# Low halves of 24 weight panels by a negation and an accumulating transfer, in place of VectorE's subtraction

## The chip, the cores and the metric

The program runs on one core of a Trainium2 chip. The metric is the device time of one execution, in microseconds (us); the kernel before takes 2033.01 us, the median of three runs (2031.76 to 2034.62).

## What is computed

A two-layer encoder over 512 tokens of width 1024. Layer 0 mixes by attention, layer 1 by a gated delta rule; around each mixer stand two half-step gated feed-forward networks (FFN), with an RMS norm ahead of every part. The change touches the mixer of layer 1 alone, cut here to its core:

```
def odd_mixer(h, w_in, conv_w, a_log, dt_bias, norm_w, w_out):
    # h: (1, 512, 1024); 8 heads of 128
    q, k, v, z, b, a = split(h @ w_in)
    q, k, v = silu(causal_depthwise_conv([q, k, v], conv_w))   # 4 taps
    q, k = l2_normalize(q), l2_normalize(k)
    g, beta = decay(a, a_log, dt_bias), sigmoid(b)
    o = gated_delta_rule_chunked(q, k, v, g, beta)             # scan over chunks
    return (rms_norm(o, norm_w) * silu(z)) @ w_out
```

## The kernel before

Every dense product runs on TensorE (PE) in three passes over numbers split in two: a high half that is the number rounded to the engine's format, and a low half, the rest. xh·wh, xl·wh and xh·wl are summed. Activations are kept split as `xnh` and `xnl`; weights are split on the way. `panel` (L163 to L177) fetches one panel of weights, 128 partitions by 1024 numbers (512 KB), from DRAM into a buffer `raw` by a transfer issued on SyncE (SP), copies it to `wh` on ScalarE (ACT, L174), which rounds, and subtracts on VectorE (DVE, L175): `wl = raw - wh`. There are three buffers each of `raw`, `wh` and `wl`, so the copy of a panel waits until PE has used the panel three before it, and the next load into a `raw` waits for the subtraction that read it.

The input projection of the delta rule goes by four pairs of heads. For each pair and each of the sections k, q and v `gdn_proj` calls `proj_steps`, which takes two panels (upper and lower half of the 1024 rows, called a and b below; k1b is the second panel of k of pair 1) and runs 24 matrix products with each, into two accumulators `mm`. `gdn_conv` (L919 to L937) then scales the result into `cx` on DVE (L926), takes the first tap into `cy` on ACT (L929), three more on DVE (L931), and the activation into `c` on ACT (L934, L937). The freeing of `cx` and `cy` goes in turn through ACT and DVE.

Beside the projections run the steps of the delta rule, of one pair while the next pair's panels are multiplied: `gdn_keys` (sums of squares on L962, scaled keys `kdec` on ACT, L972, products `iu`), and `gdn_base`, which inverts 32-wide triangular blocks on GpSimd (POOL): `iu` goes to DRAM and back as `lb` (issued by ACT, L1025), 31 steps of a product (L1037) and a subtraction (L1040) follow on POOL, and the result `rr` goes out by four transfers `rd<-rr`, issued by ACT (L1043), and back as `r` (L1046). There are four of these, base(0) to base(3), one for each pair; each head is scaled at the end by a factor `rs` (a power, POOL) on ACT (`on`, L1133).

Each engine works through its own list in order, and an instruction that issues a transfer waits at its place in that list, holding up what stands behind it. PE's list is written by hand as interleaved steps; on the other engines a scheduler orders the instructions by its estimate of when they are ready.

Of the kernel before, what the change touches and what calls it, by code (L numbers as in the profile page):

```python
# [10 lines left out]
F32 = mybir.dt.float32  # L11
F32R = mybir.dt.float32r
AF = mybir.ActivationFunctionType
ALU = mybir.AluOpType
# [3 lines left out]
D = 1024  # L18
# [70 lines left out]
class Ordered:  # L89


    def __init__(self, tc):
        self.tc, self.engine = tc, tc.nc.tensor
# [8 lines left out]
class Trunk:  # L102
# [4 lines left out]
    def __init__(self, ctx, tc):  # L107
        self.tc = tc
        self.nc = tc.nc
        self.const = ctx.enter_context(tc.tile_pool(name="const", bufs=1))  # L110
        self.xp = ctx.enter_context(tc.tile_pool(name="xp", bufs=1))
        self.wp = ctx.enter_context(tc.tile_pool(name="wp", bufs=4))
        self.np_ = ctx.enter_context(tc.tile_pool(name="np", bufs=2))
        self.ps = ctx.enter_context(tc.tile_pool(name="ps", bufs=2, space=bass.MemoryType.PSUM))
        self.dram = ctx.enter_context(tc.tile_pool(name="dr", bufs=1, space=bass.MemoryType.DRAM))
        self.ahead, self.pending, self.pin = [], [], None
        self.te = self.nc.tensor
        self.x = [self.xp.tile([P, T], F32, name=f"x{c}") for c in range(KC)]
        self.consts()
# [43 lines left out]
    def panel(self, src, a, b):  # L163

        if self.ahead:
            return self.ahead.pop()
        nc = self.nc
        raw = self.wp.tile([P, 1024], F32, tag="raw", name="raw", bufs=NRAW)
        v = raw[:, :a * b].rearrange("p (a b) -> p a b", b=b)
        nc.sync.dma_start(v, src)  # L170
        h = self.wp.tile([P, 1024], F32R, tag="wh", name="wh", bufs=NSPL)
        l = self.wp.tile([P, 1024], F32R, tag="wl", name="wl", bufs=NSPL)
        n = a * b
        nc.scalar.copy(out=h[:, :n], in_=raw[:, :n])  # L174
        nc.vector.tensor_tensor(l[:, :n], raw[:, :n], h[:, :n].bitcast(F32), op=ALU.subtract)  # L175
        return (h[:, :n].rearrange("p (a b) -> p a b", b=b),
                l[:, :n].rearrange("p (a b) -> p a b", b=b))  # L177

# [132 lines left out]
            pass  # L311
        return ps

    def proj_steps(self, ps, w, col, mk=None, cut=1):

        ps.extend(f() for f in mk or (self.mm_ps, self.mm_ps))
        n = T // cut
        for kh in range(2):
            h, l = self.panel(self.rows_half(w, kh, col), 4, 256)
            for i in range(cut):  # L320
                t = slice(i * n, (i + 1) * n)
                for j in range(2):
                    s = slice(j * P, (j + 1) * P)
                    for k in range(4):
                        kk = kh * 4 + k
                        xh, xl = self.xn[kk]
                        with self.placed():
                            self.mm3(ps[j][:, t], (h[:, k, s], l[:, k, s]), (xh[:, t], xl[:, t]),
                                     kk == 0 and i == 0, kk == KC - 1 and i == cut - 1)
                        yield  # L330
                    if kh + j and i == cut - 1:
                        self.slot()
        self.pin = None
# [427 lines left out]
    def gdn_proj(self, pool, Ks, sec, p, w_in, conv, half):  # L761

        ps = []
        yield from self.proj_steps(ps, w_in, sec * D + p * 256)
        for j, K in enumerate(Ks):
            tanh = (sec, p) in TANH
            K["qkv"[sec]] = self.gdn_conv(pool, ps[j], sec, 2 * p + j, half if tanh else conv, tanh)
# [436 lines left out]
```

## Time and profile before

| | us |
|---|---|
| median of the runs | 2033.01 |
| the profiled execution | 2032.96 |
| its span in the trace | 2031.2 |
| PE busy in the span | 1999.0 (98%) |
| DVE busy | 1084.6 (53%) |
| ACT busy | 748.3 (37%) |
| POOL busy | 130.9 (6%) |
| projections and delta rule of layer 1 | about 1324 to 1660 of the span |

In the trace a matrix product of 512 columns follows the one before it after some 0.23 us where nothing is waited for. In a timeline row stand the start, the length, engine, line, operation, what it writes and reads, and in brackets how long the engine stood idle before it and what ended that. A row "ACTq" is ACT's queue issuing a transfer. PEclk is the clock that TensorE was granted, as a share of full speed.

### The profile page before, as it was taken

The page shows a single profiled execution, that of the slowest core. Times are in us where ns is not written, and L with a number is a line of the kernel's source. Part 1 is how long each engine was busy: PE and PEld are TensorE (multiplying, and loading weights), DVE is VectorE, ACT ScalarE, POOL GpSimd, SP SyncE. Part 2 cuts the span into 40 slices and gives each one's busy share as a digit, 9 for nine tenths or more (in the row PEclk, how much of TensorE's full clock was granted, in tenths as well). Part 3 has the DMA queues.
Part 4 walks back from the last instruction along what each step waited for, and adds up shares of the span by engine and source line. Part 5 has one row for each costly group of instructions (what it writes and reads, how often), then busy time and mean ns, then how long its engine had stood idle before and what let it go on. Part 6 is the DMA issues. An engine that isn't in the chain of part 4 may idle for free.

```text
span 2031.2 us, 24843 instructions
## 1 busy us (share of the span) xinstructions
PE 1999.0 (98%) x9786; PEld 1667.5 (82%) x9786; DVE 1084.6 (53%) x1752; ACT 748.3 (37%) x1359; POOL 130.9 (6%) x298
## 2 busy tenths in 40 slices
PE   8999999999999999999999999998999999999998
PEld 7888888889888888888888888877877788888887
DVE  6452454597675433444544344478577685443543
ACT  5232233355663222233332232355465453322322
POOL 0000000100000000000000000005432400000000
PEclk9999999999999999999999999999999999999999
DMA  4333333222123333333333333234223233223332
GB/s 157 94 99 98 94 99 98 86 84 73 47 90 103 94 104 94 94 103 94 94 95 102 94 95 103 93 111 115 77 80 92 75 100 104 94 90 97 93 101 76
DMA packets 189866, 192.24 MB, mean 95 GB/s; under 512 B 28546, under 2 KB 165044, under 8 KB 189748
## 3 DMA queue, kind: packets, MB, share of 16 engines
q1 hardware_dynamic: 158916, 182.62, 28.7%
q10 hardware_dynamic: 30832, 8.02, 1.7%
q8 instruction: 77, 1.26, 0.3%
q14 instruction: 41, 0.34, 0.1%
HBM read 185.35 MB, written 5.26 MB: 94 GB/s over the span
## 4 chain that ended last, share of the span: by engine, by line
PE 89%; POOL 5%; DMA 2%; DVE 1%; issue 1%; ACT 1%; ACTq 0%; SPq 0%; POOLq 0%
PE mm L181 10%; PE mm L182 10%; PE mm L183 10%; PE pa L181 9%; PE pa L183 8%; PE pa L182 8%; PE pb L181 8%; PE pb L183 8%; PE pb L182 8%; PE mm L96 4%; POOL tmp L1037 2%; POOL rr L1040 2%; PE pb L96 1%; DMA lb<-iud 1%; DMA iud<-iu 1%
## 5 line engine op out<-in xcount | busy, mean ns | idle before, releaser
L175 DVE TENSOR_TENSOR wl<-raw,wh 128x1024 fp32r<-128x1024 f32 (+1 forms) x348 | 413.2, 1187 | 564.1 <-ACT wh L174 563.1
L174 ACT CAST wh<-raw 128x1024 fp32r<-128x1024 f32 (+1 forms) x348 | 355.6, 1022 | 702.0 <-PE pb L182 279.9
L181 PE MATMUL mm<-xnh,wh 128*128 128x512 f32 (+1 forms) x816 | 316.5, 389 | 0.6 <-ACT wh L174 0.6
L183 PE MATMUL mm<-xnh,wl 128*128 128x512 f32 (+1 forms) x816 | 317.1, 389 | 0.0
L182 PE MATMUL mm<-xnl,wh 128*128 128x512 f32 (+1 forms) x816 | 316.7, 388 | 0.0
L181 PEld LDWEIGHTS mm<-xnh,wh 128*128 128x128 f32 x816 | 154.3, 189 | 31.6 <-ACT wh L174 1.0
L183 PEld LDWEIGHTS mm<-xnh,wl 128*128 128x128 f32 x816 | 154.2, 189 | 30.5 <-issue 0.5
L182 PEld LDWEIGHTS mm<-xnl,wh 128*128 128x128 f32 x816 | 154.3, 189 | 30.4 <-issue 0.2
L181 PE MATMUL pa<-xnh,wh 128*128 128x512 f32 x400 | 156.2, 390 | 0.0
L183 PE MATMUL pa<-xnh,wl 128*128 128x512 f32 x400 | 155.8, 389 | 0.0
L183 PE MATMUL pb<-xnh,wl 128*128 128x512 f32 x400 | 155.7, 389 | 0.0
L181 PE MATMUL pb<-xnh,wh 128*128 128x512 f32 x400 | 155.7, 389 | 0.0
L182 PE MATMUL pa<-xnl,wh 128*128 128x512 f32 x400 | 155.7, 389 | 0.0
L182 PE MATMUL pb<-xnl,wh 128*128 128x512 f32 x400 | 155.7, 389 | 0.0
L226 ACT CAST hid<-hd 128x512 fp32r<-128x512 f32 x88 | 54.5, 620 | 209.0 <-DVE hd L398 209.0
L96 PE MATMUL mm<-xnh,wh 128*128 128x512 f32 x256 | 109.2, 426 | 12.0 <-DVE cx L926 12.0
L392 DVE TENSOR_TENSOR gr<-mm,rb 128x512 f32<-128x512 f32 x80 | 55.2, 691 | 94.7 <-PE mm L183 94.6
L183 PE MATMUL pb<-hid,wl 128*128 128x512 f32 x264 | 102.8, 389 | 0.0
L181 PE MATMUL pa<-hid,wh 128*128 128x512 f32 x264 | 102.7, 389 | 0.0
L182 PE MATMUL pa<-hid,wh 128*128 128x512 f32 x264 | 102.7, 389 | 0.0
L183 PE MATMUL pa<-hid,wl 128*128 128x512 f32 x264 | 102.7, 389 | 0.0
L181 PE MATMUL pb<-hid,wh 128*128 128x512 f32 x264 | 102.7, 389 | 0.0
(308 smaller groups left out, 3365.1 us busy)
## 6 DMA issues: line engine op xcount, KB each, us to landing
raw<-in_ffn_w_gate_dram SPq DMA_DIRECT2D x88, 512.0 KB, 3.6
raw<-in_ffn_w_up_dram SPq DMA_DIRECT2D x88, 512.0 KB, 3.6
raw<-in_ffn_w_down_dram SPq DMA_DIRECT2D x88, 512.0 KB, 3.6
raw<-in_gdn_w_in_dram SPq DMA_DIRECT2D x32, 512.0 KB, 3.9
raw<-in_att_w_in_dram SPq DMA_DIRECT2D x24, 512.0 KB, 3.5
raw<-in_gdn_w_out_dram SPq DMA_DIRECT2D x16, 256.0 KB, 2.7
xr<-in_x_dram SPq DMA_DIRECT2D x4, 512.0 KB, 5.6
raw<-in_att_w_out_dram SPq DMA_DIRECT2D x4, 512.0 KB, 3.4
```

The costliest lines, as they stand in the source:

```text
L96: return self.tc.keep_in_program_order(self.engine.matmul(*args, **kw))
L174: nc.scalar.copy(out=h[:, :n], in_=raw[:, :n])
L175: nc.vector.tensor_tensor(l[:, :n], raw[:, :n], h[:, :n].bitcast(F32), op=ALU.subtract)
L181: self.te.matmul(out, lhsT=lh, rhs=rh, start=start, stop=False)
L182: self.te.matmul(out, lhsT=lh, rhs=rl, start=False, stop=False)
L183: self.te.matmul(out, lhsT=ll, rhs=rh, start=False, stop=stop)
L226: nc.scalar.copy(out=h, in_=src)
L392: nc.vector.tensor_tensor(gr, g[j], self.rb, op=ALU.mult)
L1037: nc.gpsimd.tensor_tensor(p, rr[:, :k, j:j + 1].broadcast_to(sh), lb[:, j, j + 1:].rearrange("p (o m) -> p o m", o=1) .broadcast_to(sh), o ...
L1040: nc.gpsimd.tensor_tensor(rr[:, :k, j + 1:], rr[:, :k, j + 1:], p, op=ALU.subtract)
```

## The change

For the sections q, k and v of the input projection (24 panels: 4 pairs, 3 sections, 2 halves) the subtraction on DVE is left out. ACT writes `-wh` into `wl` (a second pass over the panel), and POOL issues a transfer from SBUF to SBUF that adds `raw` to it. The panels of the gate, of the output projection, of attention and of the FFNs keep the subtraction.

```
 def panel(self, src, a, b):
         nc.scalar.copy(out=h[:, :n], in_=raw[:, :n])
-        nc.vector.tensor_tensor(l[:, :n], raw[:, :n], h[:, :n].bitcast(F32), op=ALU.subtract)
+        if self.by_dma:
+            nc.scalar.activation(l[:, :n], h[:, :n].bitcast(F32), AF.Copy, scale=-1.0)
+            nc.gpsimd.dma_start(l[:, :n].bitcast(F32), raw[:, :n], accum_op=ALU.add)
+        else:
+            nc.vector.tensor_tensor(l[:, :n], raw[:, :n], h[:, :n].bitcast(F32), op=ALU.subtract)
...
-    def proj_steps(self, ps, w, col, mk=None, cut=1):
+    def proj_steps(self, ps, w, col, mk=None, cut=1, by_dma=False):
...
+            self.by_dma = by_dma
             h, l = self.panel(self.rows_half(w, kh, col), 4, 256)
+            self.by_dma = False
...
-        yield from self.proj_steps(ps, w_in, sec * D + p * 256)
+        yield from self.proj_steps(ps, w_in, sec * D + p * 256, by_dma=True)
```

In the changed file the lines of the delta rule stand 7 further down (L1037 is L1044); the negation is L177, the transfer L178. PE's list is the same row for row. DVE's has 24 instructions fewer, ACT's and POOL's 24 more each, and the scheduler has put several rows of ACT and DVE elsewhere.

First place: ACT ahead of the first `kdec` (L972, L979). Before:

```order
L904 ACTIVATE egl<-on 128x4 x2
L174 CAST wh<-raw 128x1024
L901 ACTIVATE du_10341<-du_10341 128x512
L962 ACTIVATE gosq,sk<-pa 128x128 x3
L901 ACTIVATE du_10351<-du_10351 128x512
L907 ACTIVATE kdc<-kdc 128x4x2
L904 ACTIVATE egl<-on 128x4
L962 ACTIVATE gosq,sk<-pa 128x128 x4
L934 ACTIVATE c<-cy 128x512
L904 ACTIVATE egl<-on 128x4
L962 ACTIVATE gosq,sk<-pa 128x128
```

The three rows that follow it are `cy` (L929), the cast of a panel and the first `kdec`. Now, up to the first `kdec`:

```order
L911 ACTIVATE egl<-on 128x4
L969 ACTIVATE gosq,sk<-pa 128x128
L936 ACTIVATE cy<-cx,half 128x512
L969 ACTIVATE gosq,sk<-pa 128x128 x3
L175 CAST wh<-raw 128x1024
L969 ACTIVATE gosq,sk<-pa 128x128
L177 ACTIVATE wl<-wh 128x1024
L969 ACTIVATE gosq,sk<-pa 128x128
L936 ACTIVATE cy<-cx,half 128x512
L941 ACTIVATE c<-cy 128x512
L979 ACTIVATE kdec<-pa,kd 128x128 x4
```

A negation, and one `cy` with its `c` that stood behind, come ahead of `kdec`; the sums of squares are spread among them.

Second place: POOL inside base(0), from its 20th step (75 numbers a partition). Before:

```order
L1037 TENSOR_TENSOR tmp<-rr,lb 128x75
L1040 TENSOR_TENSOR rr<-rr,tmp 128x5x15
L1037 TENSOR_TENSOR tmp<-rr,lb 128x70
L1040 TENSOR_TENSOR rr<-rr,tmp 128x5x14
L1037 TENSOR_TENSOR tmp<-rr,lb 128x65
L1040 TENSOR_TENSOR rr<-rr,tmp 128x5x13
```

Now:

```order
L1044 TENSOR_TENSOR tmp<-rr,lb 128x75
L1047 TENSOR_TENSOR rr<-rr,tmp 128x5x15
L178 DMA wl<-raw 128x1024
L1044 TENSOR_TENSOR tmp<-rr,lb 128x70
L1047 TENSOR_TENSOR rr<-rr,tmp 128x5x14
L1044 TENSOR_TENSOR tmp<-rr,lb 128x65
L1047 TENSOR_TENSOR rr<-rr,tmp 128x5x13
L178 DMA wl<-raw 128x1024
```

The transfers of v1a and v1b stand between the steps; that of q1b stands in the same way after the seventh step, those of q2b, v2a and v2b in base(1), those of k3a (after the 24th step, `rr` of 48 numbers) and k3b in base(2), none in base(3).

Third place: ACT at base(1)'s `rd<-rr`. Before:

```order
L929 ACTIVATE cy<-cx,conv 128x512
L1121 COPY on<-pb 128x128
L1125 ACTIVATE gosr,gss<-on 128x128 x2
L937 ACTIVATE c<-cy 128x512
L174 CAST wh<-raw 128x1024
L1121 COPY on<-pb 128x128 x2
L1125 ACTIVATE gosr,gss<-on 128x128 x2
L1043 DMA rd<-rr 32x8x32 x4
L929 ACTIVATE cy<-cx,conv 128x512
```

Now:

```order
L944 ACTIVATE c<-cy 128x512
L175 CAST wh<-raw 128x1024
L177 ACTIVATE wl<-wh 128x1024
L1128 COPY on<-pb 128x128 x2
L1132 ACTIVATE gosr,gss<-on 128x128 x2
L936 ACTIVATE cy<-cx,conv 128x512
L1128 COPY on<-pb 128x128 x2
L1132 ACTIVATE gosr,gss<-on 128x128
L175 CAST wh<-raw 128x1024
L1132 ACTIVATE gosr,gss<-on 128x128
L1050 DMA rd<-rr 32x8x32 x4
L1140 ACTIVATE on<-on,rs 128x128 x4
```

The `cy` that stood behind the four transfers stands ahead of them now; four scalings `on`, a `c` and another `cy` stand between them and `r<-rd`. At base(0)'s `rd<-rr` ten `cy` of the projections stand ahead in both. At base(2)'s, twelve copies `on` (L1121, now L1128) stand ahead in place of ten.

## Rows read from the trace of the kernel before

**Rows 1.** The page: engine busy times; the two groups of the split.
```profile
PE 1999.0 (98%) x9786; PEld 1667.5 (82%) x9786; DVE 1084.6 (53%) x1752; ACT 748.3 (37%) x1359; POOL 130.9 (6%) x298
...
L175 DVE TENSOR_TENSOR wl<-raw,wh 128x1024 fp32r<-128x1024 f32 (+1 forms) x348 | 413.2, 1187 | 564.1 <-ACT wh L174 563.1
L174 ACT CAST wh<-raw 128x1024 fp32r<-128x1024 f32 (+1 forms) x348 | 355.6, 1022 | 702.0 <-PE pb L182 279.9
```

**Rows 2.** Waits of PE, 1280 to 1680: in total, times, longest.
```profile
PE mm L96 <- DVE cx L926: 12.0, 3, 6.5
PE pa L99 <- ACT on L1133: 3.3, 3, 2.5
PE pa L96 <- ACT kdec L972: 2.6, 1, 2.6
```

**Rows 3.** Stretches: length, PE, PEld, DVE, ACT, POOL busy; PEclk, DMA share, GB/s.
```profile
1360.00:1380.00 20.00, 17.44 (x101) 15.11 (x100) 18.34 (x56) 13.36 (x45) 2.01 (x2) 1.00 0.61 160
...
1400.00:1420.00 20.00, 13.51 (x59) 10.84 (x58) 10.83 (x17) 6.99 (x17) 10.97 (x28) 0.88 0.31 86
...
1460.00:1480.00 20.00, 15.18 (x71) 12.41 (x70) 10.40 (x22) 7.30 (x22) 10.91 (x30) 0.83 0.21 57
```

**Rows 4.** Timeline of ACT: the first `kdec`.
```profile
1367.42 1.14 ACT L972 ACTIVATE kdec<-pa,kd 128x128 f32<-128x128 f32 x4
```

**Rows 5.** Timelines of POOL (base(0): step 1, a slow row, step 20) and ACT behind it.
```profile
1381.34 0.24 POOL L1037 TENSOR_TENSOR tmp<-rr,lb 128x31 f32<-128x31 f32 x1 [14.08 <-DMA lb<-iud]
...
1389.19 1.17 POOL L1040 TENSOR_TENSOR rr<-rr,tmp 128x66 f32<-128x66 f32 x1
...
1399.22 0.66 POOL L1040 TENSOR_TENSOR rr<-rr,tmp 128x75 f32<-128x75 f32 x1
...
1413.12 1.82 ACTq L1043 DMA_DIRECT2D rd<-rr  x4
1415.04 0.72 ACT L929 ACTIVATE cy<-cx,conv 128x512 f32<-128x512 f32 x1 [11.99 <-issue]
```

**Rows 6.** Timeline of PE: first product with v1a's `wl`; the long wait.
```profile
1396.47 0.40 PE L96 MATMUL mm<-xnh,wl 128*128 128x512 f32 x1
...
1417.20 0.80 PE L96 MATMUL mm<-xnh,wh 128*128 128x512 f32 x1 [6.49 <-DVE cx L926]
```

**Rows 7.** Timelines of ACT and PE behind base(1), and PE's next scan.
```profile
1472.25 0.72 ACT L929 ACTIVATE cy<-cx,conv 128x512 f32<-128x512 f32 x1 [9.19 <-DMA rd<-rr]
...
1475.59 0.80 PE L96 MATMUL mm<-xnh,wh 128*128 128x512 f32 x1 [4.82 <-DVE cx L926]
1476.18 0.63 PE L96 MATMUL mm<-xnl,wh 128*128 128x512 f32 x1
1476.61 0.63 PE L96 MATMUL mm<-xnh,wl 128*128 128x512 f32 x1
...
1485.92 0.89 PE L96 MATMUL pb<-t,iu 32*32 32x32 f32 x32
```

**Rows 8.** Timelines in base(2): POOL, DVE; PE's first product with k3a's `wl`.
```profile
1521.28 1.17 POOL L1040 TENSOR_TENSOR rr<-rr,tmp 128x65 f32<-128x65 f32 x1
1526.80 0.28 POOL L1040 TENSOR_TENSOR rr<-rr,tmp 128x48 f32<-128x48 f32 x1
...
1520.99 1.28 DVE L175 TENSOR_TENSOR wl<-raw,wh 128x1024 fp32r<-128x1024 f32 x1 [0.16 <-ACT wh L174]
...
1528.63 0.40 PE L96 MATMUL mm<-xnh,wl 128*128 128x512 f32 x1
```

**Rows 9.** Transfers by kind: times, KB each, median us from issue to landing.
```profile
raw<-in_gdn_w_in_dram SPq DMA_DIRECT2D x32, 512.0 KB, 3.9
...
iud<-iu ACTq DMA_DIRECT2D x8, 256.0 KB, 2.4
...
out_dram<-xt SPq DMA_DIRECT2D x4, 512.0 KB, 2.7
```

**Rows 10.** Timeline of POOL: one operation outside the bases.
```profile
1333.01 1.01 POOL L160 TENSOR_TENSOR rt<-ms,halfFalse 128x4 f32<-128x4 f32 x1 [350.45 <-DVE ms L278]
```

More of the change, by code (lines that the diff above doesn't have):

```diff
@@ L318, in proj_steps @@
         for kh in range(2):
+            self.by_dma = by_dma
             h, l = self.panel(self.rows_half(w, kh, col), 4, 256)
+            self.by_dma = False
             for i in range(cut):
```

## The prediction

> **What bounds the kernel now.** I read the page first, then PE's waits in the projection stage of layer 1, then timelines around each wait. PE is busy for 98% of the span; the split of the weights by ACT (1.02 us a panel) and DVE (1.19 us a panel) runs beside it [rows 1]. So taking 24 subtractions from DVE (24 x 1.19 = 28.5 us) and giving 24 negations to ACT (24 x 1.02, by the cast of the same size, = 24.5 us) is worth nothing by itself. What counts is what it does to PE's few waits in the stage: three behind `cx`, 12.0 us together, three behind `on`, 3.3, one behind `kdec`, 2.6 [rows 2]. The two long ones are of one kind. ACT reaches the issue of `rd<-rr` and stands there until POOL has ended a base; a `cy` behind it starts only then, after an idle time of 12.0 us at base(0) and 9.2 at base(1) [rows 5, 7]; DVE's `cx` waits for the buffer and PE for `cx`, 6.49 and 4.82 us [rows 6, 7]. After each, PE runs slower: the products behind the second follow each other by 1476.61 - 1476.18 = 0.43 us [rows 7] where two before the first wait stand closer than their 0.40 us of length [rows 6] (0.23 us is the usual step), and the granted clock of those stretches is 0.88 and 0.83 [rows 3], the lower of the levels 1.2 and 2.4 GHz for part of them. I count 12 and 13 such products: 12 x 0.2 = 2.4 us and, less the last partial one, 2.3.
>
> POOL is idle for nearly all of the span [rows 1], but not here: it takes from 1381.3 to 1413.1 for base(0) [rows 5], and its list is what the new transfers stand in.
>
> **What a low half costs now.** Until now it is ready 1.2 us after the cast. Now: a negation (1.0), POOL's turn, POOL's own time for the transfer, and the landing. No row shows an accumulating transfer or one that POOL issues. POOL's time: the low bound is ACT's issue, 1.82 us for four, 0.46 each [rows 5]; the high one is a slow operation of POOL, 1.17 [rows 5]; I take 1.0, that of its one-off power operation [rows 10]. The landing: the nearest row is a transfer of the same 512 KB out of SBUF, 2.7 us; 256 KB out of SBUF take 2.4. The high bound is a load of 512 KB and such a store one after the other, 3.9 + 2.7 = 6.6 [rows 9]. The accumulation fetches two streams and writes one, so I take 2 x 2.7 = 5.4 us, with 2.4 and 6.6 for the range. From POOL's turn to a finished `wl` that makes 6.4 us.
>
> A panel whose transfer POOL can take at once is then ready 1.0 + 6.4 - 1.2 = 6.2 us later than now. The spare time between the subtraction's end and PE's first use is 1528.63 - 1522.27 = 6.36 us for k3a [rows 8]; v1a has about as much, the other 22 panels more. So a plain delay of all panels is just hidden, with little left. What is not hidden is POOL's place: a transfer in the middle of a base waits for the steps ahead of it.
>
> **Part by part** (shifts against the profiled execution, 2032.96 us, which lies 0.05 under the median; its span is 1.8 shorter).
>
> *kdec.* Ahead of the first `kdec` [rows 4] ACT now has two negations (one of them far up, in the order of the first place) and a `cy` (0.72) with its `c` (0.6) that stood behind: 2 x 1.02 + 1.3 = 3.3 us more. About half a microsecond of idle time in front takes some; I put +2.8 us on PE's wait, making 5.4. ACT is busy for 13.4 of these 20 us [rows 3], so the low bound is nothing, and the high one 3.3. A wait of 5 us brings the slow products that the 4.82 us wait brings; I take 2.0. Together +4.8. The issue of `iud<-iu` moves less, since what was between the two `kdec` has gone ahead: base(0) starts 1.8 us later, at 1383.1.
>
> *base(0).* Now v1a's transfer stands behind step 20. In the trace this step ends at 1399.22 + 0.66, 18.5 us after the start [rows 5]. One transfer (q1b) stands ahead (+1.0). Two slow operations of POOL go: the one of 1.17 us started 0.3 us after a subtraction of DVE did, as in base(2), where 1.17 at 1521.28 follows a subtraction at 1520.99 [rows 5, 8]; without it I put 0.3, so 0.9 less each, 1.8 for two. The transfer's turn is done at 1383.1 + 18.5 + 1.0 - 1.8 = 1400.8 with 1.0 of its own still to come in the 6.4: `wl` at 1407.2 or so. PE wants it at 1396.47 + 4.8 = 1401.3 [rows 6]: a **new wait of 6.0 us**. The base, with three transfers (+3.0), ends at 1413.1 + 1.8 - 1.8 + 3.0 = 1416.1, so the wait behind `cx`, which ended at 1417.20, would end at 1420.2. PE would come there at 1417.20 - 6.49 = 1410.7, plus 10.8, 1421.5: that wait is gone. The slow products go with it and come with the new one. Running sum: 4.8 + 6.0 - 6.5 = **+4.3**.
>
> *base(1).* In the third place `cy` has gone ahead of `rd<-rr`. The 4.82 us and the 2.3 of slow products go: -7.1. The four `on`, `c` and `cy` that now stand ahead of `r<-rd` make `r` late, and PE comes earlier to the scan that reads `t`, made of `r` (1485.92 [rows 7]). With that scan at 1485.9 + 4.3 - 7.1 = 1483.1 and base(1) done at 1470.4 + 4.3, some 10 us for issue, two transfers (1.7 and 2.9 us of landing), the rows between and the turn of `t` leave 1.4 us of a new wait. Sum: 4.3 - 5.7 = **-1.4**.
>
> *base(2).* k3a's transfer stands behind step 24, which ends at 1526.80 + 0.28 [rows 8]; two slow operations less (1.7) make 1525.3, and `wl` is there at 1531.7 against 1528.63: a new wait of 3.1 us, with 1.5 of slow products. The copies that ACT now does ahead of `rd<-rr` bring `rs` and `on` earlier; of the 3.3 us behind `on` [rows 2] I take back 0.8. Sum: -1.4 + 4.6 - 0.8 = **+2.4**.
>
> *The rest.* base(3) has no transfer. The first panels and those behind the bases find POOL free. `raw` is free one landing later than now, and is not reloaded before some 7 us on. PE's list is the same. That gives 2032.96 + 2.4 = 2035.4, say **2035**, no change that can be measured: 0.2%, 4 us, is about what a measurement of this kernel can tell, so "the same" is 2028.9 to 2037.1.
>
> **Rivals.**
>
> *Cheap and covered: faster, 2028.* The landing is that of a plain store, 2.7 us [rows 9], and ACT's extra work falls into its idle third, so `kdec` costs nothing. base(0) ends 1.2 us later (three transfers less two slow operations), and the `cx` wait with it, which swallows v1a's wait; base(1) gives its 5.7; k3a waits for 1525.3 + 3.7 - 1528.63 = 0.4; `on` gives 0.8. Sum: 1.2 - 5.7 + 0.4 - 0.8 = -4.9. For it speaks that the engines move little at base(0) (share 0.31 [rows 3]); against it, that the new order ahead of `kdec` is plain to see.
>
> The Trainium skill, page "DMA: Bandwidth & Descriptors", section "Anatomy of one DMA — SWDGE (gpsimd) path", fits a transfer issued by GpSimd with 2.0 us plus the bytes by 436 thousand per us; for 512 KB that is an estimate of 3.2 us. No row here shows one. With 3.2 in place of 5.4 and `kdec` as in my forecast, the sum would be -2.6, some 2030, between this rival and the forecast.
>
> *Transfers in each other's way: slower, 2047.* The accumulation shares the DMA engines with the loads of `raw` (the share is 0.61 at 1360 to 1380 [rows 3]). If each lands behind one load, 5.4 + 3.9 = 9.3 us [rows 9], v1a and k3a wait 3.9 us longer each, and a low half comes 10.1 us later than now, more than some eight panels have to spare; three buffers let a group of neighbours wait once, so I estimate 4 us for them. Sum: 2.4 + 7.8 + 4 = +14. It decides from a landing of about 6 us on, where k3a's 6.36 us are used up without POOL's part in it. For it: the thin margin. Against: half of these stretches' DMA time is free.
>
> *The accumulation can't keep up: 2080 and more.* PE uses a panel up in 24 products of 0.23 us, 5.4 us, and three buffers allow about three times that from cast to use. With a landing over 12 us every panel waits, some 2 us or more on 24 panels. Only an operation unlike any row would do that.
>
> **How the numbers follow.** Forecast 0.40 (its own range 2030 to 2039: 0.33 the same, 0.07 slower); cheap 0.27 (0.22 faster, 0.05 the same); in each other's way 0.25; can't keep up 0.08. Faster 0.22, same 0.38, slower 0.40. The range goes from 2025 (the cheap case with `kdec` even a little earlier, and base(1) without its new wait) to 2056 (the crowded case with the estimated part doubled and slow products behind it); the last rival and thin ends are left out.
>
> **What would show it.** DVE has 24 rows of L175's kind less, ACT 24 negations of about 1.0 us. PE's wait behind `kdec` near 5 us; a wait of PE behind v1a's transfer in place of the 6.49 us at 1410.7; none behind `cx` at base(1), a short one behind `t` or `r` after it; one of 3 us at k3a. The landing of `wl<-raw` in the table of transfers decides between the cases: under 3.5 us speaks for the cheap one, over 6 for the crowded one. I would be wrong in kind if POOL's own time for a transfer were several microseconds (the bases would end later by three times that, and PE's waits with them), or if the scheduler's moves on ACT and DVE opened a wait in a place that I took as unchanged, the first panels above all.

## The result

The changed kernel takes 2051.23 us (four runs, 2050.76 to 2051.85) beside 2032.54 (four runs) for the kernel before on the same chip: a ratio of 1.0091, with a 95% interval of 1.0079 to 1.0103. It is slower by 18.7 us. The profiled execution took 2051.85 us; its span in the trace is 2050.1, that of the kernel before 2031.2.

The page of the changed kernel: busy times; the split's two groups; the group that waits for transfers; the software queue, and the new kind of transfer.

```profile
PE 2002.1 (98%) x9786; PEld 1669.6 (81%) x9786; DVE 1058.7 (52%) x1728; ACT 770.9 (38%) x1383; POOL 148.2 (7%) x322
...
q0 software_dynamic: 3456, 12.58, 3.3%
...
L180 DVE TENSOR_TENSOR wl<-raw,wh 128x1024 fp32r<-128x1024 f32 (+1 forms) x324 | 384.0, 1185 | 559.2 <-ACT wh L175 558.5
...
L96 PE MATMUL mm<-xnh,wl 128*128 128x512 f32 x256 | 103.0, 402 | 10.3 <-DMA wl<-raw 10.3
...
wl<-raw POOLq DMA_DIRECT2D x24, 512.0 KB, 5.2
```

Beside [rows 1], DVE has 24 subtractions and 25.9 us less, ACT 24 negations and 22.6 us more, POOL 17.3 us more. PE does the same work. The time went into its waits. PE's waits in the stage (compare [rows 2]): in total, times, longest.

```profile
PE mm L96 <- DMA wl<-raw: 10.3, 4, 7.1
PE pa L96 <- DVE iu L989: 7.5, 1, 7.5
PE pa L99 <- ACT vb L1022: 7.3, 1, 7.3
PE mm L96 <- DVE cx L933: 3.8, 2, 3.4
PE pa L99 <- ACT on L1140: 2.5, 1, 2.5
PE pa L99 <- ACT gosq L1008: 1.8, 1, 1.8
PE pb L96 <- DVE t L1086: 1.4, 2, 0.9
```

With two short ones the list adds up to 35.5 us; before it was 19.8, 17.9 of it in [rows 2]. That is 15.7 of the 18.9 us by which the span grew. The remaining 3.2 are slow products behind the waits: PE's busy time grew by 3.1 us with the same instructions. PE's list is the same in both, so one product can be laid beside itself. The rows of before are in [rows 6 to 8]; here are those of after, with the products behind `kdec`, behind `vb` and behind base(2):

```profile
1372.58 1.65 PE L96 MATMUL pa<-c 128*128 128x128 f32 x6 [7.54 <-DVE iu L989]
...
1411.08 0.80 PE L96 MATMUL mm<-xnh,wl 128*128 128x512 f32 x1 [7.13 <-DMA wl<-raw]
1411.68 0.63 PE L96 MATMUL mm<-xnh,wh 128*128 128x512 f32 x1
...
1428.04 0.39 PE L96 MATMUL mm<-xnh,wh 128*128 128x512 f32 x1
...
1479.44 0.39 PE L96 MATMUL mm<-xnh,wh 128*128 128x512 f32 x1
...
1492.51 1.11 PE L99 MATMUL pa<-ident,c 128*128 128x128 f32 x4 [7.31 <-ACT vb L1022]
...
1497.26 0.89 PE L96 MATMUL pb<-t,iu 32*32 32x32 f32 x32
...
1541.17 0.50 PE L96 MATMUL mm<-xnh,wl 128*128 128x512 f32 x1 [1.00 <-DMA wl<-raw]
1548.54 0.50 PE L96 MATMUL mm<-xnh,wl 128*128 128x512 f32 x1 [1.62 <-DMA wl<-raw]
...
1558.20 0.80 PE L96 MATMUL mm<-xnh,wh 128*128 128x512 f32 x1 [3.44 <-DVE cx L933]
```

PE is 14.6 us late at v1a's first `wl` (1411.08 against 1396.47), 10.8 at the product that used to wait 6.49 us (1428.04 against 1417.20), only 3.9 at the one that waited 4.82 (1479.44 against 1475.59), again 11.3 at the scan (1497.26 against 1485.92), 12.5 at k3a, and 18.9 at the end. So both old long waits behind `cx` (at base(0) and base(1)) did go, and new ones took more than their place.

Four stretches of the changed kernel (columns as in [rows 3]): the granted clock falls at each new wait, with a mean of 0.74 to 0.92 in these 20 us: part of each is run at the lower of the two levels, 1.2 of 2.4 GHz. The last two rows are the whole stage, first before, then now: the share of the DMA engines is 0.50 where it was 0.32.

```profile
1360.00:1380.00 20.00, 12.46 (x65) 10.80 (x64) 14.17 (x48) 12.46 (x39) 5.52 (x4) 0.83 0.80 183
1400.00:1420.00 20.00, 12.87 (x45) 10.11 (x44) 8.44 (x13) 5.19 (x8) 16.38 (x40) 0.74 0.54 125
1480.00:1500.00 20.00, 12.11 (x95) 9.24 (x95) 7.31 (x15) 10.84 (x38) 6.98 (x19) 0.83 0.40 100
1540.00:1560.00 20.00, 13.94 (x60) 10.67 (x60) 4.32 (x9) 8.46 (x18) 6.12 (x12) 0.92 0.83 193
...
1320.00:1660.00 340.00, 320.14 (x1991) 264.72 (x1990) 242.50 (x557) 177.54 (x505) 110.46 (x265) 0.97 0.32 89
...
1320.00:1679.00 359.00, 323.30 (x1987) 267.09 (x1987) 218.00 (x534) 197.79 (x528) 126.19 (x288) 0.95 0.50 120
```

And the chain that the waits hang on, in timelines of POOL (first step of base(0), v1a's transfer, first step of base(1)), ACT (the issue behind base(1), the scaling `on` that waits for `rs`, and `vb`) and DVE (`r` of base(2) is turned):

```profile
1387.29 0.24 POOL L1044 TENSOR_TENSOR tmp<-rr,lb 128x31 f32<-128x31 f32 x1 [12.55 <-DMA lb<-iud]
...
1406.51 0.87 POOL L178 DMA_DIRECT2D wl<-raw  x1
...
1455.80 0.23 POOL L1044 TENSOR_TENSOR tmp<-rr,lb 128x31 f32<-128x31 f32 x1 [14.58 <-DMA lb<-iud]
...
1485.20 1.89 ACTq L1050 DMA_DIRECT2D rd<-rr  x4
1487.14 1.27 ACT L1140 ACTIVATE on<-on,rs 128x128 f32<-128x128 f32 x4 [9.11 <-POOL rs L161]
...
1491.34 1.12 ACT L1022 ACTIVATE vb<-pa,vs 128x128 f32<-128x128 f32 x4
...
1556.21 1.36 DVE L1062 STREAM_TRANSPOSE t<-r 128x512 f32<-128x512 f32 x2 [15.02 <-DMA r<-rd]
```

Base(0) starts 6.0 us later than in [rows 5], and base(1) ends 14.8 later than before (1485.2 against 1470.4, in the table below). ACT stands 9.1 us until the base and `rs` behind it are done, and `vb`, for which PE waits, comes 4.2 us after that: the `on`, `c` and `cy` of the new order stand between.

### The profile page after: what moved, and what is told of

It is laid out like the page before. It is cut to its first block, busy times and chain, and to the rows that moved or that the text cites. A ratio compares the mean times of both kernels' runs of the same rounds, so it can differ in the third digit from the quotient of the medians.

```text
span 2050.1 us, 24917 instructions
## 1 busy us (share of the span) xinstructions
PE 2002.1 (98%) x9786; PEld 1669.6 (81%) x9786; DVE 1058.7 (52%) x1728; ACT 770.9 (38%) x1383; POOL 148.2 (7%) x322
## 4 chain that ended last, share of the span: by engine, by line
PE 90%; POOL 3%; DMA 3%; issue 1%; ACT 1%; DVE 1%; ACTq 1%; SPq 0%; POOLq 0%; DVEq 0%
PE mm L186 10%; PE mm L187 10%; PE mm L188 10%; PE pa L186 8%; PE pa L188 8%; PE pa L187 8%; PE pb L186 8%; PE pb L187 8%; PE pb L188 8%; PE mm L96 5%; PE pb L96 2%; POOL rr L1047 2%; POOL tmp L1044 1%; DMA lb<-iud 1%; DMA on<-gd 1%
## 5 line engine op out<-in xcount | busy, mean ns | idle before, releaser
L180 DVE TENSOR_TENSOR wl<-raw,wh 128x1024 fp32r<-128x1024 f32 (+1 forms) x324 | 384.0, 1185 | 559.2 <-ACT wh L175 558.5
L96 PE MATMUL mm<-xnh,wl 128*128 128x512 f32 x256 | 103.0, 402 | 10.3 <-DMA wl<-raw 10.3
L401 ACT ACTIVATE sg<-gr 128x512 f32<-128x512 f32 x88 | 55.2, 628 | 128.7 <-DVE gr L399 128.7
```

What stands on the lines that cost most here:

```text
L96: return self.tc.keep_in_program_order(self.engine.matmul(*args, **kw))
L401: self.last_act = nc.scalar.activation(sg, gr, AF.Silu)
```

## The experiments

The theories when the runs were made: **theory 1**, the transfers cost, by their landing and by slowing the small transfers of the delta rule; **theory 2**, the new order on ACT and DVE, the negations and POOL's issue time cost.

The scheduler moves instructions at every edit, so an edit would be measured together with a new order. To keep the two apart, most runs pin the order: a function adds to each instruction of ACT, DVE, POOL and SyncE an edge to the one that stood ahead of it in the kernel whose order is wanted (an edge for the order of issue alone, with no waiting). What an edit adds and the lists don't name is left to the scheduler.

```
         trunk_kernel(tc, *args); pinned(tc, ORDERS)
...
def pinned(tc, orders):
    """Queue each engine's instructions in the order of a list of numbers."""
    traced = {i.name: i for i in tc.nc.cur_bb.bb.instructions}
    dep = mybir.DependencyInfo(mybir.DependencyClass.NoSync, mybir.DependencyReason.DATA)
    for text in orders:
        names = [f"I-{n}" for n in text.split()]
        names = [n for n in names if n in traced]
        for a, b in zip(names, names[1:]):
            tc.add_manual_dep(traced[b], a, dep, reason="pinned")
```

All results, with the ratio to the kernel before on the same chip (95% interval), and times on the chain, read from the timelines: the first and last POOL row of base(1), the last of base(2), and the landing of base(2)'s second `r`. The runs were made on several chips, on which the kernel before takes 2032.2 to 2033.8 us, so ratios compare better than medians.

| run | order of | low half | median | ratio | base(1) starts, ends | base(2) ends | r landed |
|---|---|---|---|---|---|---|---|
| b_rdsp | before, results issued by SP | DVE | 2030.8 | 0.9990 (0.9980 to 0.9999) | 1443.4, 1472.2 | 1530.9 | 1537.9 |
| before | itself | DVE | 2032.5 | 1 | 1443.0, 1470.4 | 1531.6 | 1538.4 |
| b_rdsp_eye | as b_rdsp, `rr<-eye` on POOL | DVE | 2035.6 | 1.0012 (1.0003 to 1.0021) | 1442.7, 1471.5 | 1534.5 | 1542.2 |
| b_rdsp_free | the scheduler's own | DVE | 2035.8 | 1.0016 (1.0007 to 1.0026) | 1442.9, 1471.8 | 1533.5 | 1540.7 |
| x_order | changed | DVE | 2036.8 | 1.0017 (1.0008 to 1.0027) | 1447.9, 1477.5 | 1536.3 | 1543.8 |
| e_negdve | changed | negation, then DVE | 2037.8 | 1.0026 (1.0017 to 1.0036) | 1448.6, 1478.7 | 1537.0 | 1545.1 |
| x_small | changed | negation, 64 columns by transfer | 2039.5 | 1.0029 (1.0018 to 1.0041) | 1448.3, 1477.1 | 1535.2 | 1545.0 |
| x_bsmall | before | the same | 2040.4 | 1.0033 (1.0020 to 1.0046) | 1446.5, 1473.8 | 1534.7 | 1544.5 |
| b_rdsp_scan | the scheduler's own, first scan later | DVE | 2040.4 | 1.0034 (1.0021 to 1.0048) | 1443.8, 1473.5 | 1537.5 | 1545.7 |
| e_out | changed | transfer, outside the bases only | 2040.3 | 1.0037 (1.0023 to 1.0051) | 1451.9, 1480.0 | 1537.5 | 1544.5 |
| e_place | changed, 8 transfers earlier | transfer | 2047.9 | 1.0068 (1.0051 to 1.0084) | 1454.4, 1483.8 | 1542.2 | 1554.3 |
| changed kernel | itself | transfer | 2051.2 | 1.0091 (1.0079 to 1.0103) | 1455.8, 1485.2 | 1543.1 | 1556.8 |
| x_bfull | before | transfer | 2056.2 | 1.0112 (1.0096 to 1.0127) | 1462.5, 1489.7 | 1551.2 | 1563.1 |
| e_dead | changed | DVE, and a transfer that nobody reads | 2059.0 | 1.0125 (1.0107 to 1.0144) | 1458.0, 1489.4 | 1549.3 | 1563.9 |

### The new order alone

The kernel before, pinned to the order of the changed one (less its 24 negations and 24 transfers):

```
-        trunk_kernel(tc, *args)
+        trunk_kernel(tc, *args); pinned(tc, ORDERS)
```

> The subtraction of before, with every other instruction of ACT, DVE, POOL and SyncE pinned to the order that it has in the changed kernel; no negation and no transfer, so this is the new order alone. Theory 1 (the cost is the transfers: PE waits for their landing, and they slow the small transfers of the delta rule that share the DMA engines): the order by itself costs nothing, or even gains, since cy stands ahead of rd<-rr at base(1), which was worth 7 us; 2024 to 2034. Theory 2 (the cost is the new order on ACT and DVE, the negations and POOL's issue time): most of the 18.6 us are still there, 2040 to 2051, with the waits of PE behind kdec (over 5 us) and behind vb after base(1) (7 us).

Measured 2036.75, ratio 1.0017: between the two theories' ranges and in neither. PE's waits:

```profile
PE pa L96 <- DVE iu L982: 7.9, 1, 7.9
PE mm L96 <- DVE cx L926: 6.0, 3, 3.4
PE pa L99 <- ACT vb L1015: 4.4, 1, 4.4
```

Two things follow. The long wait at `kdec` is there without a single negation, 7.9 us against 7.5 in the changed kernel: the order alone is enough for it. And the gain at base(1) is not kept: PE gains 7.2 us on the kernel before at `cx` (the wait of 4.82 and its slow products), and gives 7.2 back by a wait of 4.4 for `vb` with slow products behind.

### Small transfers, and full ones in the order of before

```
-            nc.gpsimd.dma_start(l[:, :n].bitcast(F32), raw[:, :n], accum_op=ALU.add)
+            nc.gpsimd.dma_start(l[:, :64].bitcast(F32), raw[:, :64], accum_op=ALU.add)
```

> The changed kernel with its own order pinned, word for word, and each accumulating transfer cut from 1024 columns to 64 (the other 960 columns of those low halves are left as -wh). Negations, POOL's issues and all places are as in the changed kernel; only the bytes go. Theory 1: the landing falls from 5.2 to about 2 to 2.5 us and the small transfers land as before; PE's waits for v1a, k3a, k3b go or shrink under 3 us, vb's wait and the one at the end of base(2) go; 2026 to 2037. Theory 2: 2044 to 2051.

> The changed kernel's work (negations, full accumulating transfers), with every other instruction of ACT, DVE, POOL and SyncE pinned to the order of the kernel before. Theory 1: the transfers cost in this order too: 2043 to 2056, with lb<-iud and r<-rd landing 2 us or more later where they meet a transfer; the waits behind cx at base(0) and base(1) are back. Theory 2: without the new order little is left, the negations and POOL's issues alone: 2033 to 2041.

> As the last one, in the order of the kernel before, with the transfers cut to 64 of 1024 columns (the other columns of those low halves are left as -wh). Theory 1: 2030 to 2037, since 24 negations on ACT and 24 issues on POOL lie beside PE. Theory 2: 2033 to 2041, the same as with full transfers to within 2 us.

With 64 columns a transfer lands in 2.3 us by the median in place of 5.2, and PE's wait for `wl` is 0.3 us in all:

```profile
wl<-raw POOLq DMA_DIRECT2D x24, 32.0 KB, 2.3
```

2039.5 against 2051.2: nearly 12 us hang on the bytes in the changed order, and in the order of before 2040.4 against 2056.2, nearly 16. The order of before, which theory 2 would have had cheaper, comes out no cheaper (1.0112 beside 1.0091, with intervals that touch). With small transfers neither theory's numbers held: 2039.5 lies between the ranges, with the wait for `vb` still at 5.5 us, and 2040.4 is within theory 2's range but 16 us, not 2, from the full transfers. So the bytes are the larger part, and theory 2 is left with what x_order and x_small show, some 3.5 and 6 us over before. The full transfers in the old order make PE wait in other places:

```profile
PE mm L96 <- DVE cx L933: 10.3, 2, 6.0
PE pa L96 <- ACT kdec L979: 8.9, 1, 8.9
PE mm L96 <- DMA wl<-raw: 6.9, 3, 3.6
```

The wait for `kdec`, 2.6 us before, is 4.9 with small transfers in this order and 8.9 with full ones: the new order is not the only thing that lengthens it.

### Negation without transfer

```
-            nc.gpsimd.dma_start(l[:, :n].bitcast(F32), raw[:, :n], accum_op=ALU.add)
+            nc.vector.tensor_tensor(l[:, :n], l[:, :n].bitcast(F32), raw[:, :n], op=ALU.add)
```

> All pinned to the order of the changed kernel: the negation on ACT stays, and DVE adds raw to it in place of the transfer; no transfer, no issue on POOL. The order alone took 2036.8, the small transfers 2039.5. If the 2.8 us between these two are ACT's 24 negations: 2038.5 to 2041; if they are POOL's issues: 2036 to 2038.

2037.8 us lies in the range said for POOL's issues, but 1.0026 lies between the order alone (1.0017) and the small transfers (1.0029), and all three intervals overlap. How the step of some 2 us from the order to the small transfers divides between negations and POOL's issues is not settled.

### A transfer that nobody waits for

The subtraction stays, and behind it the same bytes move into `raw`, which is dead by then:

```
+            nc.vector.tensor_tensor(l[:, :n], raw[:, :n], h[:, :n].bitcast(F32), op=ALU.subtract)
-            nc.scalar.activation(l[:, :n], h[:, :n].bitcast(F32), AF.Copy, scale=-1.0)
-            nc.gpsimd.dma_start(l[:, :n].bitcast(F32), raw[:, :n], accum_op=ALU.add)
+            nc.gpsimd.dma_start(raw[:, :n], h[:, :n].bitcast(F32), accum_op=ALU.add)
```

> Subtraction on DVE as before, all else pinned to the order of the changed kernel, and on POOL at the changed kernel's 24 places an accumulating transfer of the same 512 KB that nobody reads: wh is added to raw after the subtraction. PE waits for no transfer, but the traffic and POOL's issues are there. The new order alone took 2036.8 us, the changed kernel 2051.2. If the slowing of the other transfers is what costs (traffic): 2043 to 2050. If PE's own waits for wl (10.3 us in the changed kernel, and the slow products behind) are what costs: 2036 to 2041.

2058.96, slower than the change itself, and more than either expectation. PE waits for no `wl` here, so its own wait for the low half is not needed for the loss. But the run is not as clean as I meant it: `raw` is reloaded only when the transfer has landed, and ACT then stands in front of a cast until the load is there (ACT's waits):

```profile
ACT wh L175 <- DMA raw<-in_gdn_w_in_dram: 9.6, 1, 9.6
```

It has DVE's subtractions beside the transfers too, and its base(0) takes 34.5 us against 32.0 in the changed kernel. So it shows that transfers at these places can cost over 20 us without PE waiting for one; it does not price traffic by itself.

### Only the 16 panels outside the bases, and the eight others moved

In e_out the eight panels whose transfers stand between POOL's steps are subtracted again; in e_place all 24 are transfers, and the eight are issued 0.3 to 2.3 us after their negation. In the changed kernel v1a's negation ended at 1398.33 and its transfer was issued at 1406.51, 8.2 us later; over the eight it is 2.6 to 9.6 us, and 0.3 for the other 16.

```
+KEEP = [((0, p), 1) for p in (1, 2)] + [((2, p), kh) for p in (1, 2) for kh in (0, 1)] + [
+    ((1, 3), 0), ((1, 3), 1)]
...
-            self.by_dma = by_dma
+            self.by_dma = by_dma and (by_dma, kh) not in KEEP
...
-        yield from self.proj_steps(ps, w_in, sec * D + p * 256, by_dma=True)
+        yield from self.proj_steps(ps, w_in, sec * D + p * 256, by_dma=(sec, p))
```

That is the edit of e_out; `KEEP` names the eight by section, pair and half. In e_place only the list of POOL's order differs.

> The changed kernel's order pinned, with the eight panels whose transfers stand inside a base on POOL (q1b, v1a, v1b, q2b, v2a, v2b, k3a, k3b) back on DVE's subtraction; the other 16 keep negation and transfer at their places. If POOL's place inside the bases is what costs: 2036 to 2042, no wait of PE for wl. If it is the traffic wherever it stands: about 16/24 of the difference between full and small transfers remains, 2045 to 2048, with lb<-iud of base(1) still landing over 5 us.

> The changed kernel with everything pinned but the place on POOL of the eight transfers that stand inside a base: each is put where POOL stood when its negation ended, or one step later (q1b after 4 steps of base(0), v1a after 12, v1b after 14; q2b after 1 step of base(1), v2a after 9, v2b after 15; k3a after 21 steps of base(2), k3b after 25). In the changed kernel these eight start 2.6 to 9.6 us after their negations, the other 16 by 0.3. If the late start is what costs: 2038 to 2043, near the kernel in which the eight are subtracted (2040.3). If the traffic inside the bases costs wherever it starts: 2046 to 2052.

e_out takes 2040.3, in the first of its two ranges: as much as with small transfers. PE still waits 0.9 us for a `wl`. Sixteen full transfers cost nothing that shows beside the small ones, though `lb` of base(1) landed late there as well (the last at 1451.7, 5.6 us after its issue). So the 11 us are the eight transfers inside the bases, with their negations and POOL's issues. e_place takes 2047.9, in the range said for the traffic, ratio 1.0068 against 1.0091, with intervals that touch: by the medians the late issue is worth less than half of the 11. PE's waits in it:

```profile
PE mm L96 <- DVE cx L933: 10.9, 3, 5.2
PE pa L99 <- ACT vb L1022: 8.1, 1, 8.1
PE pa L96 <- DVE iu L989: 7.4, 1, 7.4
```

No wait for a transfer is left (10.3 us in the changed kernel), and the time comes back behind `cx` and `vb`, that is, behind the chain: base(1) ends at 1483.8 in place of 1480.0 in e_out, base(2) 4.7 us later than there, and its second `r` lands 12.1 us after that end, against 7.0 in e_out. With small transfers at the changed kernel's places it is 9.8, with no negation 7.5. So of these 5 us about half go with the bytes (k3b's and q3a's transfers and the load behind them move just then) and half with what x_small has too. That the bytes do it by slowing `rd` and `r` is read from the landings; no run shows it alone.

### Taking ACT out of the way of the results

If the old waits come from ACT standing at `rd<-rr`, another engine can issue it. The edit of all four runs; b_rdsp and b_rdsp_eye are pinned to the order of before:

```
-            nc.scalar.dma_start(self.blocks_of(G["rd"], q, 4), rr[s])
+            nc.sync.dma_start(self.blocks_of(G["rd"], q, 4), rr[s])
...
-            nc.scalar.dma_start(K["r"].rearrange("p (t s) -> p t s", s=P), self.rows_of(G["rd"], j))
+            nc.sync.dma_start(K["r"].rearrange("p (t s) -> p t s", s=P), self.rows_of(G["rd"], j))
```

In b_rdsp_scan and b_rdsp_eye, besides:

```
-    ("scan", 0, 91.5, 1.91), ("turned", 1, 134.5, 1.09), ("gated", 0, 152.5, 1.33),
+    ("scan", 0, 97.5, 1.91), ("turned", 1, 134.5, 1.09), ("gated", 0, 152.5, 1.33),
...
-        nc.scalar.copy(out=rr, in_=G["eye"])
+        nc.gpsimd.tensor_copy(rr, G["eye"])
```

> The kernel before, all else pinned to its own order, with the four rd<-rr and two r<-rd of each base issued by SyncE instead of ACT, at places where SyncE's list is idle until a base ends (behind the 17th load of gdn_w_in, the first of gdn_w_out, the 27th of gdn_w_in, the 10th of gdn_w_out). If it is ACT standing at the issue that makes PE's waits of 6.5 and 4.8 us behind cx and the slow products after them (16 us in all): 2017 to 2026. If cx comes late for another reason, or the time is lost again at the next wait: 2030 to 2036.

> The kernel before with rd<-rr and r<-rd issued by SyncE, in the scheduler's own order, and the first scan put 6 steps later into PE's list (97.5 for 91.5). With rd on SyncE alone, PE gained 8 us at cx and gave most of it back at the scan's first product, which waited 4.2 us for t with slow products behind. If that wait is only a matter of the scan's place: 2020 to 2029. If the time is bound by base(0) itself and comes out again further on: 2029 to 2035.

> The kernel before with rd<-rr and r<-rd issued by SyncE and the scheduler left free to order ACT, DVE, POOL and SyncE (PE's list is the same as before). In the run with the order pinned this gave 2030.8, with PE's gain at cx handed on to waits for t and vb. If what counts is when a base's result lands, as the lag of PE at base(2)'s r suggests in all runs so far, the time follows that landing: within 3 us of the pinned one, 2027 to 2034, as long as base(2)'s r lands near 1538. If ACT's standing still was the cost: 2016 to 2025, since nothing pinned holds ACT's list back any more.

> As the kernel before with rd<-rr and r<-rd on SyncE (order pinned, 2030.8 us), and the copy rr<-eye moved from ACT to the head of each base on POOL. In that run ACT stood still again, 10.0 and 6.3 us in front of this copy, which waits until rd<-rr has read rr; vb, for which PE waited 3.7 us, stood behind it. If ACT's standing still is what PE pays at base(1): vb's wait goes, with the slow products after it, and 2024 to 2029. If base(1)'s end on POOL is what counts (rs, and behind it on and vb): 2029 to 2033.

With the order pinned it takes 2030.82 us, ratio 0.9990 (0.9980 to 0.9999), the one version that beats both kernels, by 2 us of the 16 looked for, and in the second of its two ranges. PE's waits:

```profile
PE pb L96 <- DVE t L1055: 4.2, 1, 4.2
PE pa L99 <- ACT vb L1015: 3.7, 1, 3.7
PE pa L99 <- ACT on L1133: 2.5, 1, 2.5
```

The long waits behind `cx` are gone (0.9 us in all is left at the projections), and PE stands at the scan of base(0) for `t`, and behind base(1) for `vb`. ACT stood still again, now in front of `rr<-eye`, which refills the one buffer `rr` and waits for `rd<-rr` to have read it:

```profile
1418.99 0.41 ACT L1032 COPY rr<-eye 128x256 f32<-128x256 f32 x1 [10.02 <-DMA rd<-rr]
```

Moved to POOL, the copy frees ACT, the wait for `vb` goes, and the next waits open at the scans (3.7 us for `t`, 2.4 for `pp`, 2.5 more for DVE) and at `cx` (2.4): 2035.57, ratio 1.0012. The free order gave 2035.82 (1.0016): the scheduler put `rr<-eye` ahead of the `cy` for which PE then waits 8.5 us. A scan put later gave 2040.44 (1.0034), with a wait of 8.2 us for the scan's own `vb`; but its order was the scheduler's too, `rr<-eye` stood ahead of `cy` there as well (7.7 us of PE's waits), so it does not test the scan's place by itself. These three lie outside both of their ranges. In the two pinned runs PE was 7.9 and 8.9 us ahead of the kernel before at the end of base(0), and 10 us later 0.1 and 1.5.

## Why the prediction went as it did

The range held the time (2025 to 2056), but the forecast was "no change", 2035, and it came out 16 us above that. The upper end of the range came from a rival whose landings of 9.3 us did not come (below); that the range held is in part luck. The misses can be placed by PE's lag: the start of a product less its start in the kernel before, in us, for products that start there at 1385, 1430, 1490, 1536 and 1550. Ahead of `kdec` the lag is -1.0 to 0.1 in these runs.

| | ahead of base(0) | behind base(0) | behind base(1) | behind k3b | behind base(2)'s `r` |
|---|---|---|---|---|---|
| forecast, running sum | 4.8 | 4.3 | -1.4 | 3.2 | 2.4 |
| x_order | 7.6 | 4.4 | 4.7 | 4.6 | 4.0 |
| e_out | 7.0 | 4.1 | 6.3 | 6.3 | 5.1 |
| e_place | 8.5 | 6.7 | 10.8 | 10.8 | 16.0 |
| changed kernel | 7.6 | 8.4 | 11.5 | 14.6 | 18.6 |

The forecast misses most at base(1), where it took 5.7 us off and 3.1 came on, and next behind base(2), 4.0 on where it took 0.8 off. Step by step:

**The price of a low half: near, a microsecond too high.** The negation takes 1.06 us (1.02 said) and POOL's time for a transfer is 0.88 (1.0 said). From the start of POOL's instruction to the landing it is 5.2 us by the median (4.5 to 8.4), and that holds POOL's 0.88; I had 6.4, since I added POOL's time to a landing that is counted from the issue. By the fit of the Trainium skill, page "DMA: Bandwidth & Descriptors", section "Anatomy of one DMA — SWDGE (gpsimd) path", the estimate was 3.2 us. The shortest of the 24 here took 4.5, and 32 KB took 2.3 by the median: the fixed part is near its 2.0; the part by bytes, 2.9 us for the 480 KB between, is more than twice its 1.1, and the measurement decides.

**kdec: the place was right, the cause not.** Said +4.8 with the slow products, and it was 6.6 by PE's lag. A wait of 1.8 behind `gosq`, which I had not looked for, came on top ahead of base(0). I put the first down to two negations and a `cy`. In x_order there is no negation, and PE waits 7.9. The chain of waits of the changed kernel in 1360 to 1375 and ACT's timeline show what came last:

```profile
1361.89 5.10 DMA on<-gd
...
1367.02 0.21 ACT L911 ACTIVATE egl<-on 128x4 f32<-128x4 f32 x1 [2.56 <-DMA on<-gd]
```

`egl`, which waits for it, stands in ACT's list ahead of six of the eight sums of squares; before, one stood behind it. In x_order ACT's idle time in front of it is 3.2 us. I had read the order of instructions that take time and not asked of one that takes 0.2 us whose transfer it waits for. No run moved `egl` alone, so this is read from the chain.

**base(0): the new wait right, its start not.** v1a's transfer did make PE wait (7.13 us, 6.0 said), and the old wait of 6.49 did go. That the two numbers are so near is luck: POOL's turn came at 1406.5 where I had 1400.8, the landing took 4.5 us where I had 6.4, and PE came 2.7 us later than I said. The base's length is 32.0 us against 31.8 (33.0 said). But it started 6.0 us late, where I had 1.8: `kdec` was 3.6 us late by the issue of `iud<-iu`, and the last `lb<-iud` took 6.0 us to land (4.8 before). In x_order, with no transfer, it started 4.2 late.

**base(1): the step that failed.** I wrote "base(1) done at 1470.4 + 4.3" and a new wait of 1.4. It was done at 1485.2. It started 12.8 us late (4.9 in x_order) and took 29.4 us in place of 27.4. The sum left its length as it was, though three transfers stand in it as in base(0), where it counted them; x_order, with none, took 29.6, so the added 2 us are not shown to be theirs. The 7 us at `cx` were gained (PE's lag falls from 8.8 to 1.6), and 7.31 of waiting for `vb` plus slow products took them back, with more (lag 11.4). x_order shows that the order alone does this, with no transfer at all: base(1) ends 7.1 us late there, and the gain becomes a wait of 4.4 us. I had priced the wait I saw, and not the one hidden under it: in x_order, as in the changed kernel, PE freed from one wait stood at the next instruction that hung on the same base. b_rdsp says the same of the kernel before.

**base(2): half.** k3a's wait was 1.0 and k3b's 1.6, with 3.1 us of lag together, where I had 4.6 for k3a's with its slow products and nothing for k3b. What I missed is behind it: the second `r` landed 18.4 us later than in the kernel before and 13.7 after the base's end (6.8 before), and PE waited 3.44 us for a `cx` that stood behind its turn on DVE.

**The rivals.** "In each other's way", 2047, is nearest in time and had the right neighbourhood, but not its price: the landings of `wl` did not rise to 9.3 us (5.2 by the median, 8.4 at most). What landed late was `lb`, `on`, `rd` and `r` (up to 7.4, 5.5, 5.9 and 6.7 us, against 4.8, 4.4, 1.7 and 4.0 before), in stretches that the transfers share. How much of the 7 us between e_out and e_place is that traffic, and how much POOL's issues and the wait for negations, no run separates.

The sum as measured, then: some 3 to 4 us for the new order, a further 2 to 4 with the negations, POOL's issues and the sixteen other transfers (not divided by any run), and some 11 for the eight panels with transfers inside the bases, of which the late issue is the smaller part by the medians. Between e_out and the changed kernel the lag grows by 3.7 us over base(0), 0.9 over base(1), 3.1 over k3a and k3b and 5.2 behind base(2)'s `r`; issued early (e_place), the eight make no wait at k3a and k3b, but 6.4 behind base(2)'s `r`. Shown by runs: the order, the bytes, and that the eight and not the sixteen cost. Argued from traces alone: that the rest of the eight's cost runs through the chain. The table of all results speaks for it: in all fourteen rows the median follows the landing of base(2)'s second `r` to within 2.5 us (+18.7 with +18.4 in the changed kernel, +15.4 with +15.9 in e_place, +26.5 with +25.5 in e_dead). It does not tell which of the two draws the other: PE's lag moves the next base's start as well.

## What to carry to other kernels

A transfer waits its turn in the list of the engine that issues it: between the steps of a chain on POOL it started 2.6 to 9.6 us after its input was ready, elsewhere 0.3, and what hangs on its landing (the product, the release of its source, the next load) was late with it. The eight that stood so cost some 11 us and the sixteen others nothing that shows; but issuing the eight earlier won back less than half, so ask also what else moves and waits in those stretches. A wait seen in a profile is worth its length only until the next wait on the same late result: before counting it as a gain, ask when the chain it waits on is done, and where the engine that waited comes to it next. And where a scheduler reorders at every edit, pin the order and change one thing, or the order is measured along with it.

## What the runs showed that was not expected

An instruction of 0.2 us on ACT (`egl`) with a transfer in front of it stands, by the chain, at the head of a wait of PE of 7.5 us, 2.6 before. A transfer of 128 KB (`lb<-iud`) that took 3.5 us by the median landed up to 7.4 us after its issue (up to 6.0 with small transfers and 6.3 with none, in b_rdsp, so other traffic has its part), and the four of 32 KB behind base(2) took up to 5.9 where they took 1.5 to 1.7. Taking away 12 us of waits of PE behind `cx` in the kernel before gave 2.
